# Where weight splits, key tiles and the last token tile's norm and row list stand in the queues of a transformer block

## Chip, cores, metric

One Trainium2 chip; the program runs on one of its cores. The metric is the device time of one execution in microseconds (us). TensorE is called PE (its weight loads PEld), VectorE DVE, ScalarE ACT, GpSimd POOL, SyncE SP.

## The reference

Two blocks over 1024 tokens of width 1024 in float32. The first (gated mixing, a state-space branch, cross attention) is not touched. The second adds to x, in turn: a gated sum of a linear recurrence and a differential attention, a cross attention to 256 memory tokens, and a mixture of 32 experts, two for each token:

```python
q = rope_partial(rms_norm(q, q_norm), cos, sin) * (ATTN_HEAD_DIM ** -0.5)
k = rope_partial(rms_norm(k, k_norm), cos, sin)
sc = einsum('bqhmd,bkhmd->bhmqk', q, k)      # 8 heads, two maps m each
p = softmax(where(mask, sc, NEG_INF))
w = p[:, :, 0] - lam * p[:, :, 1]
o = einsum('bhqk,bkhd->bqhd', w, v)
mixed = sigmoid(g_lru) * y_lru + sigmoid(g_attn) * (o_attn @ w_attn_o)
x = x + mixed @ w_out
x = x + memory_cross_attention_2(x, mem, ...)
h = rms_norm(x, norm_ffn)
# top group of 4, top 2 of its 8 experts per token, then for each expert's tokens
gu = xb @ w_gate_up[e]
y = (silu(gu[:, :512]) * gu[:, 512:]) @ w_down[e]
x = x + weight * y
```

## The kernel before

Every product is made in three matmuls of split operands: a float32 value is split into a high part (ACT copies it, `wh`, `xh`) and a low part (DVE subtracts, `wl`, `xl`). `split` does that; `mm3` issues the three matmuls (lines 173 to 175). So each weight that streams in costs a DMA on SP's queue into a raw buffer, one ACT copy and one DVE subtraction, before PE can use it.

The program is written as one trace; a planner then orders each engine's instructions by their place in the trace among those that its own timing model holds ready. On the chip each engine runs its list in order. `tc.issue_after(ins)` keeps what is issued in its block behind `ins` on the engine of `ins`. Buffers of one tag are a ring, given out in the order of the trace.

**Attention** (`attention`, marks from 690 to 1440 us) works on four pairs of heads, p = 0 to 3. A unit is (pair, query tile, head): `unit_qk` makes two score maps on PE (lines 1504 to 1509), their maxima on DVE and two exponentials on ACT (`e<-sc,st,ss`), `unit_mix` joins the two maps on DVE, `unit_tr` transposes and splits, `unit_pv` multiplies by V. A pair has 16 units, query tiles in the order 0, 7, 1, 6, 2, 5, 3, 4; each step issues the scores of the next unit ahead of the product of this one. In between, `fill` draws on the generator `fillers`: query tiles of the pair, gate units (`gate_unit`, 24 matmuls into `pg`; two units share one weight, streamed by `gate_w`), and `k_tiles` of the next pair, which projects eight key and eight value tiles (`proj`, into `pj`; `norm_rope` normalises a key tile on ACT, DVE and POOL). Weights come by `stream`, each into a raw ring `wr` of two buffers and rings `wh`, `wl` of four; `w2` streams one projection's weight in two parts. A tuple that the generator yields is a hold: nothing more is drawn until the unit loop has put it into `done`. ("k", p + 1) comes when the last unit of pair p has been issued, ("v", p + 1) after that unit's product. Key weights and value weights are streamed ahead of the first hold, and all key tiles are projected behind it.

**The mixer** (cross attention, 1650 to 1860) goes over eight token tiles in steps s1 to s10 written out by hand. For the last tile, `step(9)` writes out the order: s8 in two halves (line 166 adds to x, ACT squares with a sum into `rs3` and `ms`), then loads ahead for the experts, then s9 (transposes for the router; the sum `rs`; `rows`: h = x * norm on DVE, its write to the row buffer x3d on POOL's queue at line 1991, x's write to the output on SP's), then s10 (logits `plg`) and `route`: root of the mean square (two instructions, one on POOL), top group, top two, rank by matmuls, the list of rows per expert (`lst`, cast to `lsti` at line 2150), and behind that the softmax weights and counts. The three gather buffers `xg` are set to zero on POOL in s6 of step 8 (line 2061).

**The experts** (`moe`) take 96 gathered rows each. Six raw loads of 1 MB per expert run on SP through a ring of 15 slots (`moe_ahead`, `moe_load`); `parts` splits half a load, NP = 4 halves ahead of the matmuls. `gather` (line 2215) fetches rows by `lsti` on POOL's queue, `x_turn` transposes them (line 2232), `x_split` splits; `up`, `gated`, `a_turn`, `a_split`, `down`, `scaled` (y on ACT), `scatter` follow. The first four halves are split right after the first three gathers in the trace.

The lines that the change moves:

```python
for t in self.xg:
    nc.gpsimd.memset(t, 0.0)                       # 2061
...
if i == 7 and q:
    last = self.tt(rs3[:, 7:8], rs3[:, 7:8], self.ms[:, 0:1], OP.add)
S[i]["hT"] = hT
with tc.issue_after(last.ins) if i == 7 else nullcontext():
    rows(i)
...
for n in range(NP):
    ahead(n)                                       # moe
```

Of the kernel before, what the change touches and what calls it, by code (L numbers as in the profile page):

```python
# [11 lines left out]
F32 = mybir.dt.float32  # L12
# [4 lines left out]
AF = mybir.ActivationFunctionType  # L17
OP = mybir.AluOpType
AX = mybir.AxisListType
# [5 lines left out]
EPS = 1e-6  # L25
# [104 lines left out]
class Model:  # L130
# [906 lines left out]
    def lru(self):  # L1037
# [3 lines left out]
        self.tab = [D.tile([128, 1024], F32, name=f"ta{i}") for i in range(16)]  # L1041
        self.x0 = None
        self.w4p = self.pool("w4")
# [155 lines left out]
    def attention(self):  # L1199
# [4 lines left out]
        with self.pool("at1") as T1, self.pool("at") as T, \  # L1204
# [9 lines left out]
            alone = [False, 0]  # L1214

            def w2(src):
                return [self.stream(W, src[j], [128, 4, 256]) for j in range(2)]

# [53 lines left out]
            def gate_w(j):  # L1272
                if j < 16 and j not in gst:
                    g, n = gates[j]
                    gst[j] = self.stream(W, A["w_gl2" if g == 0 else "w_ga2"][n], [128, 8, 128])

# [20 lines left out]

            def k_tiles(p):
                wk = w2(A["w_k2"][p])
                wv = w2(A["w_v2"][p])  # L1300
                yield "k", p
                kh = T.tile([128, 4, 1024], F32R, name="kh", tag="kh")
                kl = T.tile([128, 4, 1024], F32R, name="kl", tag="kl")
                V = T.tile([128, 8, 2, 2, 128], F32R, name="V", tag="V")
                KV[p] = [kh, kl, V]
                pend = []

                def finish():
                    j, d = pend.pop(0)
                    pt = transposed(d)  # L1310
                    q = slice(j * 128, j * 128 + 128)
                    self.act(kh[:, :, q], pt, AF.Copy, scale=gcol[:, 1:2])
                    self.stt(kl[:, :, q], pt, gcol[:, 1:2], kh[:, :, q].bitcast(F32), OP.mult, OP.subtract)

                for n in range(8 + 2):
                    if n < 8:
                        o = []
                        yield from proj(wk, n, o)
                        d, _ = norm_rope(o[0], n, True)
                        pend.append((n, d))  # L1320
                    if n == 1:
                        yield "v", p
                    if n > 1:
                        j = n - 2
                        o = []
                        yield from proj(wv, j, o)
                        ps = o[0].rearrange("p (h a) b -> p h (a b)", h=2)
                        self.split(V[:, j, :, 0], V[:, j, :, 1], ps)
                        finish()
                        yield 0.3  # L1330
                        if j == 3:
                            WQ[p] = w2(A["w_q2"][p])

# [147 lines left out]
    def unit_qk(self, unit, QS, KV):  # L1481
# [37 lines left out]
        for m in range(2):  # L1519
            e = T.tile([128, 512 if one else 1024], F32, name="e", tag=f"e{m}{int(one)}", bufs=1)  # L1520
            ev = e[:, 0:W] if one else e[:, 0:W].rearrange("p (a b) -> p a b", a=2)
            self.act(ev, vs[m], AF.Exp, bias=st[:, m:m + 1], scale=rqh[:, m:m + 1], accum=st[:, 2 + m:3 + m])
            es.append(e[:, 0:W])
# [354 lines left out]
    def mixer_tiles(self, x2, XX, xxp, PQ, PT, wcq, wrt, wqp):  # L1878
# [115 lines left out]
        def s9(i):  # L1994
            hT = T.tile([128, 8, 128], F32, name="hT", tag="hT")
            for q in range(2):
                pt = transposes([x2[i][:, (4 * q + a) * 128:(4 * q + a + 1) * 128] for a in range(4)], 4)
                if q:
                    self.act(hT[:, 4:8], pt, AF.Copy)
                else:  # L2000
                    nc.vector.tensor_copy(out=hT[:, 0:4], in_=pt)
                if i == 7 and q:
                    last = self.tt(rs3[:, 7:8], rs3[:, 7:8], self.ms[:, 0:1], OP.add)
            S[i]["hT"] = hT
            with tc.issue_after(last.ins) if i == 7 else nullcontext():
                rows(i)
# [19 lines left out]
        def step(n):  # L2026
# [18 lines left out]
            for f, d in order:  # L2045
                if 0 <= n - d < 8:
# [8 lines left out]
                    if (f, n) == (s6, 8):  # L2055
# [3 lines left out]
                        self.xg = [XG.tile([BLK, 1024], F32, name=f"xg{j}") for j in range(3)]  # L2059
                        for t in self.xg:  # L2060
                            nc.gpsimd.memset(t, 0.0)
                        self.moe_ahead((self.RA, NRA), 2)
# [6 lines left out]
        with self.pool("mt7", side="right") as T, self.pool("po8", space=PSUM) as P2:  # L2069
# [4 lines left out]
            for n in range(1, 11):  # L2074
# [7 lines left out]
                if n in (3, 5, 7, 9):  # L2082

                    self.moe_ahead((self.RA, NRA), 1)

    def route(self, tiles, pl, T, P2, tag):

# [5 lines left out]
        rs = self.rs3[:, ti]  # L2093
        self.ts(rs, rs, 1.0 / 1024, OP.mult, EPS, OP.add)
        self.rsqrt(rs, rs, nb)
        lg = t("lg", 40)
# [52 lines left out]
        if tiles[-1] == 7:  # L2149
            nc.vector.tensor_copy(out=self.lsti, in_=self.lst[:, 0])  # L2150
        yield

        self.tt(ge, lg[:, :, 0:4], bc(m8[:, :, 0, 0:1], 4), OP.subtract)
        self.act(ge, ge, AF.Exp)
        nc.vector.tensor_reduce(out=f[:, :, 1], in_=ge, op=OP.add, axis=AX.X)
        nc.vector.reciprocal(out=f[:, :, 2], in_=f[:, :, 1])
        self.tt(f[:, :, 4], m8[:, :, 1, 1], m8[:, :, 1, 0], OP.subtract)
        self.act(f[:, :, 5], f[:, :, 4], AF.Tanh, scale=0.5)
        self.ts(f[:, :, 6], f[:, :, 5], -0.5, OP.mult, 0.5, OP.add)
        self.ts(f[:, :, 7], f[:, :, 5], 0.5, OP.mult, 0.5, OP.add)  # L2160

        half = f[:, :, 12]
        self.ts(half, rs, 0.5, OP.mult)
        self.tt(f[:, :, 2], f[:, :, 2], rs, OP.mult)
        self.tt(f[:, :, 2], f[:, :, 2], half, OP.mult)
        self.tt(self.val[:, ti, :, 1], f[:, :, 6:8], bc(f[:, :, 2:3], 2), OP.mult)
        nc.vector.tensor_copy(out=self.val[:, ti, :, 2], in_=f[:, :, 12:13].to_broadcast([128, nb, 2]))
        listed(1, 2)
        self.stt(self.dst[:, ti], f[:, :, 10:12], 32.0, f[:, :, 8:10], OP.mult, OP.add)
        for b in range(nb):  # L2170
            self.tt(self.cacc, self.cacc, M[:, b], OP.add)
        if tiles[-1] == 7:

            pc = P2.tile([128, 32], F32, name="pcn", tag=tag)
            nc.tensor.matmul(pc, self.one, self.cacc, start=True, stop=True)
            self.cnt = self.const.tile([128, 32], F32, name="cnt")
            nc.vector.tensor_copy(out=self.cnt, in_=pc)

# [29 lines left out]
    def moe(self):  # L2208
        nc, A, tc = self.nc, self.A, self.tc
        with self.pool("moe") as T, self.pool("mg", bufs=3, space=PSUM) as PG, \  # L2210
# [40 lines left out]
            def gated(u, c):  # L2251

                if c == 0:
                    u["t"] = T.tile([BLK, 512], F32, name="tg", tag="tg", bufs=2)
                    self.act(u["t"], u["pg", 0], AF.Tanh, scale=u["half"])
# [33 lines left out]
            def scatter(u):  # L2289
# [5 lines left out]
                  "xt": xg[e % 3]} for e in range(32)]  # L2295

            for e in range(3):
                gather(U[e])
# [55 lines left out]
            gather(U[3])  # L2354
            for n in range(NP):
                ahead(n)
            for n, (f, e, c, k) in enumerate(work):
# [196 lines left out]
```

## Time and profile before

| what | value |
|---|---|
| median of 3 runs | 2488.14 us (2485.55 to 2493.98) |
| the profiled execution's own time | 2485.62 us |
| its span on the core | 2483.9 us |
| mean granted clock of PE, share of full | 0.983 |
| PE, DVE, ACT, POOL busy | 95%, 70%, 53%, 14% of the span |
| attention | 690 to 1440 us |
| out projection, mixer | 1440 to 1650, 1650 to 1860 us |
| experts | 1860 to 2474 us |

Times in a row of the timeline are microseconds from the span's start, then the duration; what stands in brackets is the idle time of the engine before the instruction and what ended it. "x4" at the end of a row joins four like instructions. A matmul's duration overlaps the next one's. The window rows give the busy time of each engine in a stretch, the number of its instructions, PE's granted clock as a share of 2.4 GHz, the mean busy share of the DMA engines and what they moved.

### The profile page before, as it was taken

What the parts mean: (1) busy time and instruction counts of PE and PEld (TensorE: products, weight loads), DVE (VectorE), ACT (ScalarE), POOL (GpSimd) and SP (SyncE); (2) the same over time, 40 slices, a digit from 0 to 9 for tenths busy, and PEclk for the clock granted to TensorE, in tenths of its full rate; (3) what the DMA queues carried; (4) which work ended last, traced back from release to release, by engine and by line L of the source; (5) the groups of instructions that cost most, each with busy time, mean ns of one, the idle gap of its engine ahead of it and who ended that gap; (6) DMA issues with size and microseconds to landing.
All of it is one profiled execution on the core that took longest, in us unless ns stands there. A gap on an engine that the chain in (4) does not pass through costs nothing. (4 is left out here: it accounts for less than half of the span.)

```text
span 2483.9 us, 35045 instructions
## 1 busy us (share of the span) xinstructions
PE 2355.6 (95%) x13016; PEld 1936.7 (78%) x13016; DVE 1748.2 (70%) x3344; ACT 1314.5 (53%) x2102; POOL 341.5 (14%) x363
## 2 busy tenths in 40 slices
PE   8999989999999999999899899999997999999998
PEld 6888868787888898798798678887885777666765
DVE  9667767677875666666666744235667999898987
ACT  5344532445645455454445432134435888787886
POOL 1011114100021021121121100000011111111111
PEclk9999999999999999999999999999998999999999
DMA  6322353322221111110111456532267999999992
GB/s 222 99 68 67 117 179 127 123 78 84 72 77 39 64 45 42 51 52 35 56 51 40 144 199 221 176 119 77 85 244 271 368 376 373 371 372 359 368 371 66
DMA packets 103838, 394.32 MB, mean 159 GB/s; under 512 B 14129, under 2 KB 33073, under 8 KB 79089
## 3 DMA queue, kind: packets, MB, share of 16 engines
q1 hardware_dynamic: 85008, 335.18, 37.5%
q0 software_dynamic: 18656, 56.88, 7.3%
q8 instruction: 104, 1.70, 0.3%
q14 instruction: 70, 0.57, 0.1%
HBM read 339.07 MB, written 61.31 MB: 161 GB/s over the span
## 5 line engine op out<-in xcount | busy, mean ns | idle before, releaser
L166 DVE TENSOR_TENSOR wl<-raw,wh 128x1024 fp32r<-128x1024 f32 (+1 forms) x496 | 587.7, 1209 | 130.3 <-ACT wh L154 126.1
L154 ACT ACTIVATE wh<-raw 128x1024 fp32r<-128x1024 f32 (+1 forms) x496 | 512.1, 1048 | 250.0 <-PE pj L174 67.2
L173 PE MATMUL pj<-wh,xnh 128*128 128x256 f32 x768 | 222.2, 289 | 2.1 <-ACT tg L154 1.0
L175 PE MATMUL pj<-wh,xnl 128*128 128x256 f32 x768 | 217.2, 283 | 0.0
L174 PE MATMUL pj<-wl,xnh 128*128 128x256 f32 x768 | 217.0, 283 | 0.0
L175 PE MATMUL pg<-wh,xl 128*96 128x512 f32 x512 | 201.3, 393 | 1.6 <-DVE xl L166 1.6
L174 PE MATMUL pg<-wl,xh 128*96 128x512 f32 x512 | 202.6, 396 | 0.0
L173 PE MATMUL pg<-wh,xh 128*96 128x512 f32 x512 | 200.2, 400 | 0.9 <-ACT xh L154 0.9
L173 PEld LDWEIGHTS pj<-wh,xnh 128*128 128x128 f32 x768 | 145.4, 189 | 3.8 <-ACT pc L154 2.5
L174 PEld LDWEIGHTS pj<-wl,xnh 128*128 128x128 f32 x768 | 145.2, 189 | 0.0
L175 PEld LDWEIGHTS pj<-wh,xnl 128*128 128x128 f32 x768 | 145.1, 189 | 0.0
L154 ACT ACTIVATE e<-sc,st,ss 128x1024 f32<-128x1024 f32 (+7 forms) x128 | 105.7, 829 | 54.2 <-DVE st L158 42.4
L178 POOL TENSOR_TENSOR ss<-ss,mhalf 128x4 f32<-128x4 f32 (+1 forms) x68 | 72.7, 1069 | 343.5 <-DVE ss L163 318.4
L173 PE MATMUL pd<-wh,ah 128*96 128x512 f32 x248 | 98.2, 400 | 16.6 <-ACT y L154 16.6
L175 PEld LDWEIGHTS pg<-wh,xl 128*96 128x96 f32 x512 | 83.1, 162 | 38.6 <-DVE xl L166 3.2
L173 PEld LDWEIGHTS pg<-wh,xh 128*96 128x96 f32 x512 | 83.0, 162 | 33.8 <-ACT xh L154 1.3
L174 PEld LDWEIGHTS pg<-wl,xh 128*96 128x96 f32 x512 | 82.8, 162 | 32.4
L173 PE MATMUL pg<-xnh,wh 128*128 128x512 f32 x256 | 104.9, 410 | 0.4 <-ACT kv L154 0.2
L175 PE MATMUL pg<-xnh,wl 128*128 128x512 f32 x256 | 102.6, 401 | 0.0
L173 PE MATMUL pj<-xnh,wh 128*128 128x512 f32 x256 | 102.2, 400 | 0.0
L174 PE MATMUL pg<-xnl,wh 128*128 128x512 f32 x256 | 102.2, 399 | 0.0
L174 PE MATMUL pj<-xnl,wh 128*128 128x512 f32 x256 | 101.2, 396 | 0.0
(998 smaller groups left out, 6327.5 us busy)
## 6 DMA issues: line engine op xcount, KB each, us to landing
raw<-in_w_gu SPq DMA_DIRECT2D x128, 1024.0 KB, 15.3
raw<-in_w_dn SPq DMA_DIRECT2D x64, 1024.0 KB, 15.9
raw<-in_w_out SPq DMA_DIRECT2D x16, 512.0 KB, 4.6
ta<-tg POOLq DMA_DIRECT2D x32, 256.0 KB, 2.5
t<-ta SPq DMA_DIRECT2D x14, 512.0 KB, 3.9
raw<-in_w_ga SPq DMA_DIRECT2D x12, 512.0 KB, 3.7
raw<-in_w_v SPq DMA_DIRECT2D x12, 512.0 KB, 3.5
xraw<-in_xT SPq DMA_DIRECT2D x8, 512.0 KB, 5.8
```

Source lines behind the costliest of these rows:

```text
L154: return self.nc.scalar.activation(out=out, in_=in_, func=func, **kw)
L166: return (eng or self.nc.vector).tensor_tensor(out=out, in0=a, in1=b, op=op)
L173: mm(ps, l[0], r[0], start=start, stop=False)
L174: mm(ps, l[0], r[1], start=False, stop=False)
L175: return mm(ps, l[1], r[0], start=False, stop=stop)
L178: self.nc.gpsimd.tensor_tensor(out=out, in0=in_, in1=self.mhalf[:, :w], op=OP.pow)
```

## The change

In attention, the streams of `w2` and `gate_w` are issued behind the last exponential traced so far (`self.last_exp`), on ACT. The first two key tiles of a pair are projected ahead of the hold ("k", p), the value weights are streamed behind them, and the value hold comes at the third key tile. In the mixer the zeroing of `xg` becomes three ACT copies with scale 0 in s9 of the last tile, whose root is taken there too, ahead of `rows`; `route` skips it for that tile, and what it does behind the list stands behind the list's cast (`self.known`) on DVE. In the experts the first four part splits are issued behind the zeroing (ACT) and the cast (DVE), the ring of raw loads has one slot more, and `tg` one buffer instead of two.

```diff
+            def after_exp():
+                return self.tc.issue_after(self.last_exp.ins) if self.last_exp else nullcontext()
             def w2(src):
-                return [self.stream(W, src[j], [128, 4, 256]) for j in range(2)]
+                with after_exp():
+                    return [self.stream(W, src[j], [128, 4, 256]) for j in range(2)]
...
-                    gst[j] = self.stream(W, A["w_gl2" if g == 0 else "w_ga2"][n], [128, 8, 128])
+                    with after_exp():
+                        gst[j] = self.stream(W, A["w_gl2" if g == 0 else "w_ga2"][n], [128, 8, 128])
...
             def k_tiles(p):
                 wk = w2(A["w_k2"][p])
+                pend = []
+                def project(n):
+                    o = []
+                    yield from proj(wk, n, o)
+                    d, _ = norm_rope(o[0], n, True)
+                    pend.append((n, d))
+                yield from project(0)
+                yield from project(1)
                 wv = w2(A["w_v2"][p])
                 yield "k", p
...
-                for n in range(8 + 2):
+                for n in range(2, 8 + 2):
                     if n < 8:
-                        o = []
-                        yield from proj(wk, n, o)
-                        d, _ = norm_rope(o[0], n, True)
-                        pend.append((n, d))
-                    if n == 1:
+                        yield from project(n)
+                    if n == 2:
                         yield "v", p
-                    if n > 1:
-                        j = n - 2
...
+                    j = n - 2
...
-            self.act(ev, vs[m], AF.Exp, bias=st[:, m:m + 1], scale=rqh[:, m:m + 1], accum=st[:, 2 + m:3 + m])
+            self.last_exp = self.act(ev, vs[m], AF.Exp, bias=st[:, m:m + 1], scale=rqh[:, m:m + 1], accum=st[:, 2 + m:3 + m])
...
-                if i == 7 and q:
-                    last = self.tt(rs3[:, 7:8], rs3[:, 7:8], self.ms[:, 0:1], OP.add)
+                    if i == 7:
+                        self.tt(rs3[:, 7:8], rs3[:, 7:8], self.ms[:, 0:1], OP.add)
+                        root = self.root(rs3[:, 7:8], 1)
+                        for t in self.xg:
+                            self.first = self.act(t, self.ident[0:BLK, 0:1].to_broadcast([BLK, 1024]), AF.Copy,
+                                                  scale=0.0)
             S[i]["hT"] = hT
-            with tc.issue_after(last.ins) if i == 7 else nullcontext():
+            with tc.issue_after(root.ins) if i == 7 else nullcontext():
                 rows(i)
...
-                        for t in self.xg:
-                            nc.gpsimd.memset(t, 0.0)
...
+    def root(self, rs, n):
+        i = self.ts(rs, rs, 1.0 / 1024, OP.mult, EPS, OP.add)
+        self.rsqrt(rs, rs, n)
+        return i
...
-        self.ts(rs, rs, 1.0 / 1024, OP.mult, EPS, OP.add)
-        self.rsqrt(rs, rs, nb)
+        if i0 < 7:
+            self.root(rs, nb)
...
-            nc.vector.tensor_copy(out=self.lsti, in_=self.lst[:, 0])
+            self.known = nc.vector.tensor_copy(out=self.lsti, in_=self.lst[:, 0])
         yield
+        with self.tc.issue_after(self.known.ins) if tiles[-1] == 7 else nullcontext():
...
-                    u["t"] = T.tile([BLK, 512], F32, name="tg", tag="tg", bufs=2)
+                    u["t"] = T.tile([BLK, 512], F32, name="tg", tag="tg")
...
+            self.moe_ahead((T, 1), 1)
             for e in range(3):
                 gather(U[e])
...
-            for n in range(NP):
-                ahead(n)
+            with tc.issue_after(self.first.ins), tc.issue_after(self.known.ins):
+                for n in range(NP):
+                    ahead(n)
```

Under the line `with self.tc.issue_after(self.known.ins) ...` the rest of `route` is indented, unchanged.

## Rows read from the trace of the kernel before

**Rows 1.** The page's busy line: engine, busy us (share of the span), instructions

```profile
PE 2355.6 (95%) x13016; PEld 1936.7 (78%) x13016; DVE 1748.2 (70%) x3344; ACT 1314.5 (53%) x2102; POOL 341.5 (14%) x363
```

**Rows 2.** Windows: attention, head, experts; stretch, us, busy PE PEld DVE ACT POOL, PEclk, DMA, GB/s

```profile
690.00:1440.00 750.00, 714.67 (x4846) 640.53 (x4845) 485.31 (x1215) 371.03 (x759) 120.21 (x139) 0.98 0.16 57
...
1860.00:1883.40 23.40, 8.43 (x69) 7.51 (x67) 12.31 (x51) 3.64 (x8) 4.24 (x5) 0.62 0.67 241
1883.40:2473.50 590.10, 570.54 (x2683) 401.77 (x2682) 532.79 (x564) 484.86 (x571) 86.81 (x60) 1.00 0.93 339
```

**Rows 3.** Waits of PE, 690 to 1440: total us, times, longest us

```profile
PE sc L1504 <- ACT e L154: 10.5, 10, 1.9
```

**Rows 4.** Timeline of ACT in attention, end of pair 0: start, us, operation, [idle before]

```profile
805.19 1.06 ACT L154 ACTIVATE wh<-raw 128x1024 fp32r<-128x1024 f32 x1 [1.61 <-PE pg L174]
...
823.06 1.06 ACT L154 ACTIVATE wh<-raw 128x1024 fp32r<-128x1024 f32 x1 [0.94 <-PE pj L175]
...
835.05 1.06 ACT L154 ACTIVATE wh<-raw 128x1024 fp32r<-128x1024 f32 x1 [5.91 <-PE pg L174]
...
837.46 0.99 ACT L154 ACTIVATE e<-sc,st,ss 128x768 f32<-128x768 f32 x1
...
881.15 0.89 ACT L154 ACTIVATE e<-sc,st,ss 128x640 f32<-128x640 f32 x1 [1.09 <-DVE oss L166]
```

**Rows 5.** Timeline of PE at the end of pair 0

```profile
837.13 0.44 PE L1504 MATMUL sc<-kh,qs 128*128 128x384 f32 x1 [1.88 <-ACT e L154]
...
838.10 0.61 PE L173 MATMUL pg<-xnh,wh 128*128 128x512 f32 x1
...
857.84 0.37 PE L173 MATMUL pj<-wh,xnh 128*128 128x256 f32 x1
...
862.63 0.28 PE L173 MATMUL pj<-wh,xnh 128*128 128x256 f32 x1
...
865.47 0.60 PE L1538 MATMUL pt<-ident,e 128*128 128x128 f32 x4
```

**Rows 6.** Windows: from pair 0's last gate unit to its last exponential

```profile
857.70:882.00 24.30, 20.13 (x144) 18.15 (x144) 18.12 (x51) 10.98 (x25) 2.69 (x4) 0.93 0.10 33
```

**Rows 7.** Timelines of POOL, DVE, ACT and PE at the head of the experts

```profile
1846.40 2.72 POOL L2061 MEMSET xg<- 96x1024 f32 x3
1867.70 0.59 POOL L1991 DMA_DIRECT2D x3d<-h  x1 [18.58 <-DVE rs L163]
...
1877.68 1.10 POOL L2215 DMA_INDIRECT xg<-x3d,lsti  x1 [8.77 <-issue]
...
1864.98 1.22 DVE L166 TENSOR_TENSOR wl<-raw,wh 128x1024 fp32r<-128x1024 f32 x1
1866.12 0.15 DVE L166 TENSOR_TENSOR rs<-rs,ms 128x1 f32<-128x1 f32 x1
...
1868.95 0.20 DVE L166 TENSOR_TENSOR rt_u<-plg,rs 128x36 f32<-128x36 f32 x1 [1.48 <-POOL rs L178]
...
1874.30 0.18 DVE L2150 CAST lsti<-lst 96x32 int32<-96x32 f32 x1
...
1857.75 3.89 ACT L154 ACTIVATE wh<-raw 128x1024 fp32r<-128x1024 f32 x4
...
1863.79 1.03 PE L2018 MATMUL plg<-wrt,hT 128*128 128x36 f32 x8
...
1881.90 1.54 PE L2232 MATMUL pt<-ident,xg 96*128 96x96 f32 x8 [6.19 <-DMA xg<-x3d,lsti]
```

**Rows 8.** The reduce of line 1957: count, duration ns min/median/max, first and last start

```profile
L1957 DVE TENSOR_REDUCE on<-po x8: 1224/1226/2337, 1707.7 to 1846.8; 128x512 f32<-128x1024 f32 x8
```

**Rows 9.** The row writes of line 1991: from issue to landing

```profile
DMA to landing us min/median/max: 2.9/2.9/3.0
```

**Rows 10.** The gathers of line 2215: duration of the issue on POOL, ns

```profile
L2215 POOL DMA_INDIRECT xg<-x3d,lsti x32: 957/1147/3049, 1877.7 to 2391.2; - x32
```

**Rows 11.** Waits of PE among the experts, 2050 to 2475

```profile
PE pd L173 <- ACT y L154: 16.6, 12, 1.7
```

More of the change, by code (lines that the diff above doesn't have):

```diff
@@ L1041, in lru @@
         self.tab = [D.tile([128, 1024], F32, name=f"ta{i}") for i in range(16)]
-        self.x0 = None
+        self.x0 = self.last_exp = None
         self.w4p = self.pool("w4")
@@ L1305, in k_tiles @@
                 KV[p] = [kh, kl, V]
-                pend = []
                 def finish():
@@ L1313, in finish @@
                     self.stt(kl[:, :, q], pt, gcol[:, 1:2], kh[:, :, q].bitcast(F32), OP.mult, OP.subtract)
-                for n in range(8 + 2):
+                for n in range(2, 8 + 2):
                     if n < 8:
-                        o = []
-                        yield from proj(wk, n, o)
-                        d, _ = norm_rope(o[0], n, True)
-                        pend.append((n, d))
-                    if n == 1:
-                        yield "v", p
-                    if n > 1:
-                        j = n - 2
[L1325 to L1332, printed above, removed]
+                        yield from project(n)
+                    if n == 2:
+                        yield "v", p
+                    j = n - 2
+                    o = []
+                    yield from proj(wv, j, o)
+                    ps = o[0].rearrange("p (h a) b -> p h (a b)", h=2)
+                    self.split(V[:, j, :, 0], V[:, j, :, 1], ps)
+                    finish()
+                    yield 0.3
+                    if j == 3:
+                        WQ[p] = w2(A["w_q2"][p])
             def q_tile(p, i):
@@ L2149, in route @@
         if tiles[-1] == 7:
-            nc.vector.tensor_copy(out=self.lsti, in_=self.lst[:, 0])
+            self.known = nc.vector.tensor_copy(out=self.lsti, in_=self.lst[:, 0])
         yield
[L2153 to L2177, printed above, removed]
+        with self.tc.issue_after(self.known.ins) if tiles[-1] == 7 else nullcontext():
+            self.tt(ge, lg[:, :, 0:4], bc(m8[:, :, 0, 0:1], 4), OP.subtract)
+            self.act(ge, ge, AF.Exp)
+            nc.vector.tensor_reduce(out=f[:, :, 1], in_=ge, op=OP.add, axis=AX.X)
+            nc.vector.reciprocal(out=f[:, :, 2], in_=f[:, :, 1])
+            self.tt(f[:, :, 4], m8[:, :, 1, 1], m8[:, :, 1, 0], OP.subtract)
+            self.act(f[:, :, 5], f[:, :, 4], AF.Tanh, scale=0.5)
+            self.ts(f[:, :, 6], f[:, :, 5], -0.5, OP.mult, 0.5, OP.add)
+            self.ts(f[:, :, 7], f[:, :, 5], 0.5, OP.mult, 0.5, OP.add)
+            half = f[:, :, 12]
+            self.ts(half, rs, 0.5, OP.mult)
+            self.tt(f[:, :, 2], f[:, :, 2], rs, OP.mult)
+            self.tt(f[:, :, 2], f[:, :, 2], half, OP.mult)
+            self.tt(self.val[:, ti, :, 1], f[:, :, 6:8], bc(f[:, :, 2:3], 2), OP.mult)
+            nc.vector.tensor_copy(out=self.val[:, ti, :, 2], in_=f[:, :, 12:13].to_broadcast([128, nb, 2]))
+            listed(1, 2)
+            self.stt(self.dst[:, ti], f[:, :, 10:12], 32.0, f[:, :, 8:10], OP.mult, OP.add)
+            for b in range(nb):
+                self.tt(self.cacc, self.cacc, M[:, b], OP.add)
+            if tiles[-1] == 7:
+                pc = P2.tile([128, 32], F32, name="pcn", tag=tag)
+                nc.tensor.matmul(pc, self.one, self.cacc, start=True, stop=True)
+                self.cnt = self.const.tile([128, 32], F32, name="cnt")
+                nc.vector.tensor_copy(out=self.cnt, in_=pc)
```

## The prediction, made before the change was built

> **What bounds the kernel now.** I read the busy line first: PE is busy for 95% of the span, DVE for 70% and ACT for 53% [rows 1]. An average like that hides stages, so the table by stage comes next [rows 2]. Attention (690 to 1440 us) has PE busy for 714.7 of 750 us: 35 us idle in all. The experts (1883.4 to 2473.5) have 570.5 of 590.1. Only the short stretch between them and the mixer is not PE's: from 1860 to 1883.4 PE works 8.4 of 23.4 us. The change touches attention and this stretch, so a gain can come from 35 us at one place and from 15 at the other, never more.
>
> In attention the longest entry in PE's waits is a score tile waiting for an exponential, 10.5 us in 10 times [rows 3]. ACT's timeline shows how this arises at the end of head pair 0: a weight split of the next pair's V (835.05, 1.06 us) sits in front of a unit's two exponentials (the second at 837.46), having waited 5.91 us for matmuls of a gate [rows 4]; PE then stands 1.88 us at 837.13 [rows 5]. That pattern comes three times, at pairs 0, 1 and 2.
>
> At the head of the experts, the chain is: sum of squares, root, logits, row list, gather, transposes, first matmul. The last tile's sum of squares is added at 1866.12, only because DVE has four `wl` parts ahead of it (the last at 1864.98) and ACT four `wh` parts, 3.89 us from 1857.75, ahead of the square; then the multiply of h sits before the root as well. The list ends at 1874.48, but the gather starts at 1877.68; the engine is held by "issue", that is by nothing that the profile names. What it reads besides the list is the row buffer, whose last write was issued at 1867.70; I infer that it waited for it. PE starts at 1881.90 [rows 7].
>
> **The change, part by part.**
>
> *Head of the experts.* (1) The three zeroings of the gather buffers leave POOL (2.72 us at 1846.40). Beside them the DVE reduce of L1957 took 2.34 us, where its others took 1.23 [rows 8]: 1.1 us comes back. ACT takes the three, priced by its like-sized copies at about 1.05 us each [rows 4], in a stretch where it works 3.6 of 23.4 us [rows 2]; they must only end before the gather. (2) With the first four splits behind zeroing and list, the square no longer waits on ACT, nor the sum on DVE: four subtractions less put the sum at 1866.12 - 4 x 1.22 = 1861.2, and I say 1861.9, since the square must end first. The root then is ready near 1863.0, and the next bound is the logits, whose eight matmuls end at 1864.82 [rows 7]. With one semaphore's delay, the first routing step goes from 1868.95 to about 1864.9: -4.0. (3) From there to the list it was 5.5 us (1868.95 to 1874.48). About ten short side operations of DVE, 0.14 to 0.2 each, now follow the list: -1. (4) The row write leaves near 1863.5 instead of 1867.70. Its duration has two bounds: 2.9 us is the landing of the writes that the trace could match [rows 9], and 1877.68 - 1868.29 = 9.4 us is what this one took if the gather waited for it. The middle of the two, 6.2, lands it near 1869.7, no later than the list, at 1869.5; so the list sets the gather. The gather would start near 1870, against 1877.68: -7.7. (5) The `wl` parts, four by 1.22 us [rows 7], now come behind the list at 1869.5 and end near 1874.4, just when the gather's rows are there (4.2 us after its start, 1877.68 to 1881.90 [rows 7]); xl may be 0 to 1.2 late; with (1)'s 1.1 I call it even. Head: **-7.6**, between -3 (write at 9.4 us: 1863.5 + 0.6 + 9.4 = 1873.5, and 1.2 late) and -9.5.
>
> Of gathers beside DVE, the row shows 0.96 to 3.05 us of POOL for one [rows 10], and the first, at 1.10, ran with a nearly idle DVE. The Trainium skill, "SBUF — State Buffer", the part on who interferes with whom, says that subtracting two SBUF operands on DVE (which the splits do) contends with GpSimd's reads, though it doesn't lock it out; by that, the first gather, now beside the four `wl`, would sit at the long end of that row, and the head's gain would be 5.7. No run here shows the overlap yet.
>
> (6) One more raw slot, one `tg` buffer less: weights lead their splits, and `tg` is reused once per expert; PE's waits in that phase name neither [rows 11]. Zero; the cover is the loads' lead. If `tg` bound, it would show as a wait on `tg`.
>
> *Attention.* (7) The streams' ACT splits now stay behind the last exponential traced. The gate weight that was split at 805.19 has to follow the exponential of 837.46 [rows 4], so the gate that starts at 838.10 [rows 5] can't start before that exponential and a split of 1.05. In return the split of 835.05 no longer delays the pair of exponentials, about 1 us. So 837.46 becomes 836.5, its end 837.4, the split's 838.4: +0.3; without the earlier start it is 839.4: +1.3. I take +0.5 a pair, nearer the first, as the split in front is plain in the row. (8) The next pair's key weights, split in two parts, the first at 823.06 [rows 4], are traced after the scores of the pair's last unit, so they must follow that unit's exponential, 881.15 + 0.89 = 882.0 [rows 4]. Two key tiles run there today, from 857.84 and from 862.63, 24 matmuls each, the second until the transposes at 865.47 [rows 5]: 2.8 us for one, so 5.6 us of PE work that can't be there any more. That they stand before the hold in the program does nothing for it: the planner already ran them ahead of the unit that ends the hold. The stretch is 24.3 us with 20.1 of PE, 18.1 of DVE [rows 6]. Without the tiles PE has 14.5 left and DVE about 16 (one tile's normalising is some 2 us), so the chain of exponentials tightens, but not by all of 5.6. Bounds: it tightens fully, 0; not at all, +5.6. I take 4 of 5.6, since 24.3 - 4 is still 4 above DVE's work, as the stretch is now 4 above PE's: loss 1.6, less a little that transposes and mixing fill. +1.5 a pair. (9) The three tiles now in a row share one PSUM buffer, whose copies take 0.4 us: within that term. Pair 3 has no successor, pair 0's start no exponential yet. The query weights' splits move behind exponentials, but the tiles that use them come much later: zero while that holds. Attention: 3 x 2.0 = **+6**, between -9 (the 1.9 us stall and half of the 4.2 us idle vanish in each pair) and +20.
>
> Sum: -7.6 + 6 = -1.6 on the profiled execution's 2485.6 (span 2483.9 and 1.7 around it): 2484.0. That execution is 2.5 below the median of 2488.1, so on the median's footing it is 2486.5. I say **2485**. A measurement of this kernel tells about 0.3%, 7.5 us, from no change.
>
> **The rivals.**
>
> *R1, attention gains too (0.34).* With no split in front, the exponentials come earlier and PE's 4.2 us of idle at each pair's end halves, and the 1.9 us stall with it: 3 x -3 = -9 at best, -3 likely. 2485.6 - 7.6 - 3 to -9: about 2472, range 2468 to 2479. For it: 10.5 us of such waits exist [rows 3]. Against: most stand in the middle of pairs, where no split precedes.
>
> *R2, PE starves at the pair's end (0.17).* The chain of exponentials at 857.7 to 882 doesn't tighten, since it is its own latencies, and PE idles where the two tiles were. +5.6 and 0.5 to 1.3 a pair, some +19: 2485.6 - 7.6 + 19 = 2497. It decides once more than 5 us a pair is lost, from about 2495.6 on. For it: at 881.15 the exponential itself waits for DVE. Against: DVE and PE are shared by tiles and chain now.
>
> *R3, another order of the planner in the experts (0.06).* PE waits 12 times, 1.7 us at most, for y's scaling, 16.6 us in all [rows 11]; another order of ACT's queue there could add half as many or as many again, 8 to 17: at +12, 2485.6 - 7.6 + 6 + 12 = 2496.
>
> *The change does nothing in attention* is 2478.0 on the execution's footing and 2480.5 on the median's, at the forecast's edge to R1; I give it no chance of its own, since splits that start before the exponential of 881.15 are what the edit forbids.
>
> **How the numbers follow.** Forecast 0.43 (within 0.3%), R1 0.34 (faster), R2 and R3 0.23 (slower). The likeliest's own range is 2480.6 to 2495.6. The range 2471 to 2499 takes in most of R1, R2's and R3's centres, and the bounds of head and tiles short of their joint ends.
>
> **What would show it.** In the profile after: the first matmul of the experts some 7.6 us closer to the logits' end; the gather directly behind the list's cast; `wl` and `wh` parts behind it. In attention, gate units 8, 16 and 24 starting right after a split that follows an exponential; the first key tile of pairs 1 to 3 only behind the pair's last exponential; PE's busy time from the gate's end to that exponential about 14.5 us in some 20. Wrong would be: key splits still ahead of the last exponential, a gather that still waits with the list ready, or a stretch of 24 us with 14.5 of PE in it (R2).

## The result, and the profile after

The changed kernel takes 2516.79 us (median of 4 runs, 2512.48 to 2519.76); the kernel before, beside it, 2486.85. The ratio is 1.0119, with a 95% interval of 1.0102 to 1.0136: 1.2% slower, where no measurable change was forecast (2485, range 2471 to 2499).

Where the 30.6 us of the span (2483.9 to 2514.5) went is read by setting the same events of both traces side by side:

| from - to | before | after |
|---|---|---|
| start to the first key projection of attention | 694.7 | 697.2 |
| from there to the end of attention's last transposes | 742.7 | 773.5 |
| from there to the end of the last logits | 427.4 | 425.0 |
| from there to the first expert matmul | 18.6 | 18.5 |
| from there to the end of the last expert matmul | 589.7 | 590.5 |

The 2.5 us at the start lie in unchanged code (that stretch took between 691.8 and 699.1 us in the runs below). Attention lost 30.8, out projection and mixer gained 2.4, and the head of the experts, where -7.6 was forecast, gained next to nothing. The windows of the kernel after, in the columns of [rows 2] and shifted to the same work, say it for the engines:

```profile
692.50:1473.40 780.90, 726.94 (x4846) 642.91 (x4846) 488.06 (x1215) 370.35 (x759) 120.41 (x139) 0.98 0.16 55
1890.90:1914.10 23.20, 7.92 (x67) 7.45 (x66) 13.03 (x48) 4.07 (x9) 8.31 (x6) 0.68 0.77 275
```

Attention issues the same work (4846 matmuls, 759 ACT instructions) in 30.9 us more. PE's idle time grew from 35.3 to 54.0, and the same matmuls were busy 12.3 us longer. PE's mean granted clock is 0.98 in both rows, so the clock does not account for that.

Where the time went shows when each pair's turn is cut in two: from its first exponential to the end of its last, and from there to the first exponential of the next pair. Pair 0, before and then after:

```profile
759.47:882.03 122.56, 116.30 (x715) 100.01 (x714) 78.39 (x198) 58.61 (x126) 13.60 (x17) 0.97 0.13 44
882.03:938.96 56.93, 56.89 (x480) 56.41 (x479) 37.39 (x101) 30.73 (x65) 14.43 (x17) 1.00 0.17 57
```

```profile
761.99:880.35 118.36, 109.60 (x652) 91.54 (x650) 71.98 (x184) 54.75 (x121) 13.06 (x16) 0.99 0.09 32
880.35:948.40 68.05, 65.17 (x541) 64.15 (x542) 44.33 (x115) 34.26 (x68) 15.62 (x18) 1.00 0.21 71
```

The first part became 4.2 us shorter and the second 11.1 us longer: 8.3 us more of PE's work and 2.8 us more of idle time. What moved is 64 projection matmuls (`pj`), two key tiles and two thirds: the first part has 120 instead of 184, the second 456 instead of 392. At pairs 1 and 2 the first part is 2.4 and 3.7 us shorter, the second 12.7 and 12.9 us longer. Together these are 26.4 of the 30.8 us. The rest lies in pair 3, where no key tiles follow; the new place of the key tiles alone, measured below, shows the same 4.3 us there.

The waits of PE in attention, in the form of [rows 3], one row before and three after:

```profile
PE pt L1538 <- DVE e L158: 3.3, 4, 1.5
```

```profile
PE pt L1550 <- DVE e L158: 12.9, 7, 2.5
PE sc L1516 <- ACT e L154: 10.5, 15, 1.3
PE pj L173 <- ACT wh L154: 4.5, 4, 1.4
```

Scores wait for exponentials as long in all as before, 10.5 us. Transposes that wait for the mixing behind the exponentials do so for 12.9 us instead of 3.3. New are key and value tiles (`pj`) that wait for a weight's split, which none did before. ACT at the end of pair 0, to be read against [rows 4]:

```profile
838.88 0.99 ACT L154 ACTIVATE e<-sc,st,ss 128x768 f32<-128x768 f32 x1 [6.43 <-DVE st L158]
...
840.34 0.99 ACT L154 ACTIVATE e<-sc,st,ss 128x768 f32<-128x768 f32 x1
...
841.31 1.06 ACT L154 ACTIVATE wh<-raw 128x1024 fp32r<-128x1024 f32 x1
...
879.47 0.88 ACT L154 ACTIVATE e<-sc,st,ss 128x640 f32<-128x640 f32 x1
880.25 0.19 ACT L154 ACTIVATION_READ_ACCUMULATOR e<-sc,st,ss 128x1 f32 x1
880.34 1.99 ACT L154 ACTIVATE wh<-raw 128x1024 fp32r<-128x1024 f32 x2
...
886.64 1.06 ACT L154 ACTIVATE wh<-raw 128x1024 fp32r<-128x1024 f32 x1 [3.30 <-DMA raw<-in_w_v]
```

The order is what the edit asks for: the gate's split stands behind the pair of exponentials, the two parts of the key weights (880.34) behind the pair's last one. The last row was not foreseen: the value weights' split waits for its own load. The raw ring has two buffers; the key weights held both until their splits, so the value weights' load could only start then, at 883.17, where the kernel before issued it at 825.41 (SP's queue, after and before):

```profile
883.17 1.46 SPq L1634 DMA_DIRECT2D raw<-in_w_v  x2
```

```profile
825.41 4.14 SPq L1622 DMA_DIRECT2D raw<-in_w_v  x2
```

PE of the kernel after in the same stretch:

```profile
874.94 1.11 PE L1550 MATMUL pt<-ident,e 128*128 128x128 f32 x5 [2.47 <-DVE e L158]
881.44 0.38 PE L173 MATMUL pj<-wh,xnh 128*128 128x256 f32 x1 [1.14 <-ACT wh L154]
882.87 0.38 PE L1562 MATMUL po<-V,wth 128*128 128x256 f32 x1 [1.05 <-ACT wth L154]
887.75 0.50 PE L173 MATMUL pj<-wh,xnh 128*128 128x256 f32 x2 [0.70 <-ACT wh L154]
```

The first key tile of pair 1 starts at 881.44 instead of 857.84 [rows 5], though the work around it came up to 3 us earlier. The waits of 1.14 us (for the key split), 1.05 us (for a copy that ACT made behind both key splits) and 0.70 us (for the value split) are the idle time of that second part. At the head of the experts, against [rows 7] (ACT, DVE, POOL, SP, PE):

```profile
1888.71 3.89 ACT L154 ACTIVATE wh<-raw 128x1024 fp32r<-128x1024 f32 x4
...
1894.82 0.22 DVE L166 TENSOR_TENSOR lst<-lst,pls 96x64 f32<-96x64 f32 x1 [2.15 <-PE pls L2165]
1894.96 0.15 DVE L166 TENSOR_TENSOR rs<-rs,ms 128x1 f32<-128x1 f32 x1
...
1896.88 0.20 DVE L166 TENSOR_TENSOR rt_u<-plg,rs 128x36 f32<-128x36 f32 x1 [0.45 <-POOL rs L178]
...
1902.05 0.18 DVE L2171 CAST lsti<-lst 96x32 int32<-96x32 f32 x1
...
1902.50 1.22 DVE L166 TENSOR_TENSOR wl<-raw,wh 128x1024 fp32r<-128x1024 f32 x1
...
1903.70 1.22 DVE L166 TENSOR_TENSOR wl<-raw,wh 128x1024 fp32r<-128x1024 f32 x1
...
1903.20 2.67 POOL L2237 DMA_INDIRECT xg<-x3d,lsti  x1 [5.81 <-ACT rt_f L154]
...
1904.95 2.78 SPq L2209 DMA_DIRECT2D raw<-in_w_gu  x2
...
1911.67 1.54 PE L2254 MATMUL pt<-ident,xg 96*128 96x96 f32 x8 [9.88 <-DMA xg<-x3d,lsti]
```

The list comes sooner behind the logits (1902.23 - 1895.65 = 6.6 us; before 9.7) and the gather a microsecond behind the list (before 3.2). But from the gather's start to the transposes it is 8.5 us, where it was 4.2. Five microseconds were won and four of them lost there; a further one went to the rest of the list, whose matmuls (`pls`, at 1913.01) now ran between the transposes and the first expert matmul.

### The profile page after: what moved, and what is told of

Its sections match the earlier page's. It is cut to its first block, busy times and chain, and to the rows that moved or that the text cites. A ratio compares the mean times of both kernels' runs of the same rounds, so it can differ in the third digit from the quotient of the medians.

```text
span 2514.5 us, 35050 instructions
## 1 busy us (share of the span) xinstructions
PE 2371.1 (94%) x13016; PEld 1941.8 (77%) x13016; DVE 1749.2 (70%) x3344; ACT 1314.7 (52%) x2105; POOL 343.9 (14%) x360
## 5 line engine op out<-in xcount | busy, mean ns | idle before, releaser
L154 ACT ACTIVATE pc<-pj 128x256 f32<-128x256 f32 x96 | 36.3, 382 | 126.5 <-PE pj L175 116.6
```

Of the source, the lines that this page charges most:

```text
L154: return self.nc.scalar.activation(out=out, in_=in_, func=func, **kw)
```

## The experiments

All are measured beside the kernel before. Theory S: the splits tied to the last exponential traced starve PE at the end of each pair. Its rivals are named in the expectations: H (the head has a share), T (the tiles' new place costs), G (the gates' order is a large part), W (keys alone do little).

**Attention's edits alone** (the hunks of `attention`, `k_tiles`, `unit_qk`).

```diff
+    with after_exp():  # w2, gate_w
...
+    yield from project(0)
+    yield from project(1)
     wv = w2(A["w_v2"][p])
     yield "k", p
```

> Theory S (starved pair ends): the whole loss is in attention, where the out projection began 30.9 us later in the changed kernel than before (2.5 us of the shift came earlier, in unchanged code); the attention edits alone give +27 to +31 us, about 2515. Rival H (the head takes a share through DMA contention among the experts): attention alone gives less, +20 to +25, and the rest is missing.

Measured 2523.45, ratio 1.0138 (1.0118 to 1.0157): 36 us slower, above the 27 to 31 expected. Its attention takes 773.5 us, to a tenth what the changed kernel's takes, so the whole loss there is these edits'. It is 6 us slower than the changed kernel because its expert phase took 598.6 us instead of 590.5, with the same code in another order from the planner.

**The head's edits alone** (zeroing, root, `known`, part splits, slot, `tg`).

```diff
+    root = self.root(rs3[:, 7:8], 1)
...
+    with tc.issue_after(self.first.ins), tc.issue_after(self.known.ins):
+        for n in range(NP):
+            ahead(n)
```

> The head's edits alone. Theory S: the list's gain of 3 us is given back by a gather that is slower beside the weight loads and the splits, so -1 to +1 us, about 2486, the first expert matmul 18.5 us behind the end of the logits. Rival H: +4 to +8 us. The forecast of the prediction: -7.6.

Measured 2487.91, ratio 1.001 (0.9995 to 1.0025): no difference. First expert matmul 18.1 us behind the logits.

**The order alone** (`after_exp` without the key tiles' new place) and **the key tiles' new place alone**.

```diff
+    with after_exp():  # first kernel
...
+    yield from project(0)  # second kernel
+    yield from project(1)
     wv = w2(A["w_v2"][p])
     yield "k", p
```

> The splits behind the last exponential, without key tiles ahead of the hold. Theory S: this order alone starves PE, so +24 to +30 us, with no key tile of pairs 1 to 3 before the last exponential of the pair ahead. Rival T (the tiles' new place takes the time): under +12.

> Only the key tiles ahead of the hold (and the value weights' stream behind them, the value hold one tile later), no order between splits and exponentials. Theory S: within 5 us of the kernel before, since the planner already ran two key tiles ahead of the hold. Rival T: +12 or more.

The order alone: 2514.72, ratio 1.0111 (1.0090 to 1.0132). The tiles alone: 2480.45, ratio 0.9961 (0.9945 to 0.9977), faster by 6.9 us where at most 5 were expected. So the change holds a gain of 0.4% and a loss that buries it. With the tiles alone, the stretch at the pair's end, where PE idled 4.2 us [rows 6], is full (windows of that kernel):

```profile
859.50:883.50 24.00, 23.36 (x187) 21.82 (x187) 19.40 (x58) 11.68 (x28) 4.10 (x5) 1.00 0.09 33
```

From a pair's last exponential to the next pair's first it is 54.6 us there at each of three pairs, before 56.4 to 57.7. No split moved: PE still stands 1.88 us ahead of the scores (at 838.92).

In the order without tiles, attention was 24.7 us longer than before (2.8 of them ahead of the first exponential, where no tie acts yet); with them, 30.8. The tiles do nothing for the order: what they need is split behind the exponential that they were to cover.

**Only the gate weights tied**, and **all but the key weights tied** (the latter in the changed kernel).

```diff
-    with after_exp():  # w2 of the first kernel
+    wk = w2(A["w_k2"][p], True)  # second kernel: outside after_exp
```

> Only the gate weights' splits stay behind the last exponential; key, value and query weights are free, key tiles in their old place. Theory S (the loss is the key weights' order): -3 to +6 us against before, the stall of 1.88 us ahead of the scores at the pair's end shorter. Rival G (the gates' order is a large part of the loss): +10 or more.

> The changed kernel with one exception: the key weights' splits are free of the order. Theory S: at least 18 of the 30 us come back, so 2480 to 2499, and key tiles stand ahead of the pair's last exponential again. Rival G: 2505 or more.

Gates: 2504.12, ratio 1.0059 (1.0042 to 1.0076), 14 us, the rival's size. Key weights free: 2500.21, ratio 1.0048 (1.0030 to 1.0066); 17 us came back, a little short of the 18 named, and only 11.8 of them in attention (761.7 against 773.5). So neither is the whole. In the gates' kernel, the stall ahead of the scores did shrink, but two more stood behind it (PE):

```profile
837.31 0.44 PE L1509 MATMUL sc<-kh,qs 128*128 128x384 f32 x1 [0.60 <-ACT e L154]
838.77 0.44 PE L1509 MATMUL sc<-kh,qs 128*128 128x384 f32 x1 [0.33 <-ACT e L154]
841.75 0.87 PE L1543 MATMUL pt<-ident,e 128*128 128x128 f32 x6 [1.31 <-DVE e L158]
```

0.60 + 0.33 + 1.31 = 2.2 us in place of 1.88: the gate unit that ran there now waits for its weight, and nothing covers the mixing. Most of the loss stands later: PE waits 2.46 us for the mixing at 876.24 (before, 1.41 at 873.95), and 16 projection matmuls slip behind the pair's last exponential (408 instead of 392). In all of attention the waits for the mixing are 12.9 us in 7 times, as in the changed kernel. From this stall to the same one of the next pair it is 183.0 us (to 1020.32), before 179.5 (837.13 to 1016.66). With the key weights free, the value weights' splits took their place behind the last exponential. No run ties the value or the query weights alone.

**Only the key weights tied**, all else as before.

```diff
     def w2(src, tied=False):
         with after_exp() if tied else nullcontext():
...
     wk = w2(A["w_k2"][p], True)
```

> Only the key weights' splits stay behind the last exponential; everything else as before. Theory S (PE starves at the pair's end where the key tiles ran): 4 to 6.5 us at each of three pairs, +12 to +20 us; the first key tile of pairs 1 to 3 comes some 23 us later against its neighbours, the chain of exponentials only some 3 us earlier. Rival W (it needs the value and gate weights tied as well): under +6.

Measured 2514.51, ratio 1.0098 (1.0068 to 1.0128): 25 us, above the range of theory S and far from its rival. Attention (694.7 to 1460.3) has 22.9 of them; 2.7 of these lie ahead of the first exponential, where no tie acts yet and the granted clock was 0.95 instead of 1.00. At the three pairs it is 7.7, 5.1 and 6.0 us, 18.7 in all and within the range. Its windows at the end of pair 0:

```profile
858.50:882.50 24.00, 15.32 (x78) 12.29 (x77) 16.64 (x49) 11.80 (x25) 2.60 (x3) 0.76 0.02 6
882.50:905.00 22.50, 22.50 (x170) 22.39 (x170) 16.73 (x42) 11.01 (x22) 6.83 (x8) 0.87 0.38 123
```

PE has 78 matmuls in the first stretch, where [rows 6] have 144, and it idles 8.7 us instead of 4.2. The granted clock was 0.76 of full in it (1.2 GHz for part of it) and 0.87 in the next, where PE had no idle time at all and still only 170 matmuls; before, that next stretch ran at 1.00 with 198:

```profile
882.00:905.00 23.00, 23.00 (x198) 23.00 (x197) 15.52 (x47) 11.55 (x27) 9.27 (x11) 1.00 0.12 47
```

From pair to pair, at the same place as above, it is 187.2 us (838.67 to 1025.84) instead of 179.5. So the starved end costs three times in this kernel: the tiles' own time, the value weights whose load waited for the raw buffers (a split at 887.20 waited 2.92 us for it), and the clock, which was 0.95 behind the last exponential of each of the three pairs. In the changed kernel it was 1.00, 0.94 and 1.00 there.

**The whole change, tied to an earlier exponential**: that of the sixth unit back.

```diff
-    return self.tc.issue_after(self.last_exp.ins) if self.last_exp else nullcontext()
+    return self.tc.issue_after(self.exps[-7].ins) if len(self.exps) >= 7 else nullcontext()
```

> The whole change, but every split of attention stays behind the exponential of the sixth unit back instead of the last one traced. If the loss comes from which exponential it is (theory S: the last one traced belongs to the unit that ends the pair, so that the key tiles can't run beside it): 2472 to 2488, key tiles ahead of the pair's last exponential, PE's half clock after it gone. If any tie of splits to exponentials starves PE: 2500 or more.

Measured 2489.20, ratio 1.0000 (0.9989 to 1.0011): all of the loss is gone. It is a microsecond above the range named, but 27 us below the changed kernel. It is not the tie to exponentials that starves PE but which one is named. Key tiles run from 852.4 again. PE's half clock is not gone, against what I expected: it stands for 3.4 us from 877.8, behind a wait for the mixing of 3.2 us at 876.90. The gain of the tiles alone does not come with this tie. The tiles alone have no such wait there, but that it is the whole reason is not shown.

**The gather at the head.** Two variants of the head's edits: weight loads held on SP's queue, and subtractions held on DVE, until rows have landed.

```diff
+    hold = nc.sync.dma_start(out=scr[:, 0:1], in_=U[0]["xt"][:, 0:1])  # first kernel
+    seen = nc.vector.tensor_copy(out=scr[:, 0:1], in_=U[0]["xt"][:, 0:1])  # second kernel
```

> The head's edits, and the weight loads that the first four part splits release wait on their queue until the first gather has landed (a copy of one column of its rows, on the same queue, ahead of them). If the loads slow the gather: its landing falls from 8.1 us between the gather's start and the transposes (head alone) to about 6, first expert matmul 2 us earlier, 2485 to 2487. If DVE's subtractions beside it do it: nothing changes, 8 us.

> The head's edits, but the first four subtractions on DVE start only when the first gather has landed (behind a DVE copy of one column of its rows), and with them the loads. If subtractions beside the gather slow it: its issue takes 1.1 instead of 2.67 us and it is 4 to 4.5 us from its start to the transposes, first expert matmul 3 us earlier less some 1 us of waiting for the low parts: 2484 to 2487. If not: 8 us remain and the low parts come late, 2489 to 2493.

Measured 2488.07, ratio 0.9995 (0.9980 to 1.0010), and 2486.05, ratio 0.9980 (0.9965 to 0.9995). In both I had put the copy behind the fourth gather, which fills the same buffer, so it waited for that one and not for the first; in the second the low parts came 5.0 us late on PE and ate most of the gain. The first missed its range by a microsecond, the second lies in it. The first expert matmul came 15.8 and 13.5 us behind the logits instead of 18.1, but the expert phases took 594.8 and 595.9 us instead of 592.1. The gather itself can still be read. Head's edits alone (POOL, PE):

```profile
1869.94 2.67 POOL L2225 DMA_INDIRECT xg<-x3d,lsti  x1 [5.81 <-ACT rt_f L154]
...
1877.99 1.54 PE L2242 MATMUL pt<-ident,xg 96*128 96x96 f32 x8 [9.45 <-DMA xg<-x3d,lsti]
```

Loads held, subtractions beside the gather (DVE, POOL, PE):

```profile
1876.88 1.21 DVE L166 TENSOR_TENSOR wl<-raw,wh 128x1024 fp32r<-128x1024 f32 x1
...
1877.92 1.12 POOL L2225 DMA_INDIRECT xg<-x3d,lsti  x1 [7.36 <-issue]
...
1882.17 1.54 PE L2242 MATMUL pt<-ident,xg 96*128 96x96 f32 x8 [7.20 <-DMA xg<-x3d,lsti]
```

That is 8.1 us to the transposes with the head's edits alone and 4.3 with the loads held, where two loads still left at 1880.57 and 1880.95 instead of three from 1871.69 on. With both held it is 4.5 us (1876.95 to 1881.45), issue 1.08. From the end of the issue on it is 5.4 us with the loads and 3.1 without. The run with the earlier tie, which has the head's edits too, shows the two apart the other way: an issue of 1.15, then 5.5 us beside three loads.

The issue beside subtractions took 2.67 and 2.07 us with the head's edits alone, and 1.12 and 2.06 with the loads held; with neither, 1.08 and 0.99. All four end 0.86 to 0.95 us, about the length of an undisturbed issue, behind the end of a subtraction that no other follows at once. For the short one that end came at 1878.09, 0.17 us after the gather's start; for the long one of the changed kernel it came at 1904.92, 1.72 us after it. So by these rows the issue waits until DVE leaves off subtracting.

**A version that beats both**: the tiles alone, the head's edits, and the subtractions held until the first gather has landed (copy ahead of the fourth); the tiles alone with the value weights' splits behind the exponential of the sixth unit back; and the two together.

```diff
     yield from project(0)
     yield from project(1)
-    wv = w2(A["w_v2"][p])
+    with after_exp(7):
+        wv = w2(A["w_v2"][p])
...
+    seen = nc.vector.tensor_copy(out=scr[:, 0:1], in_=U[0]["xt"][:, 0:1])
     x_turn(U[0])
...
+    with tc.issue_after(self.first.ins), tc.issue_after(seen.ins):
+        for n in range(NP):
+            ahead(n)
```

> The key tiles ahead of the hold without any order behind exponentials, the head's edits, and the first four subtractions on DVE only when the first gather has landed, this time placed ahead of the fourth gather. If key tiles gain by themselves (-7) and the gather is slowed by the subtractions and the loads that they release: 2474 to 2480, 4 to 4.5 us from the gather's start to the transposes, first expert matmul 14 to 16 us behind the logits' end.

> The key tiles ahead of the hold, and the value weights' splits behind the exponential of the sixth unit back, where a split has stood in front of a pair of exponentials. If the stall of 1.88 us is that split's: 1 to 2 us less at each of three pairs than with the tiles alone, 2474 to 2480. If a later split or wait takes its place: as the tiles alone, 2480, or above.

> The two kernels before together. If their gains are at separate places: 2470 to 2477.

Measured 2478.24 (ratio 0.9951, 0.9935 to 0.9967), 2477.23 (0.9949, 0.9927 to 0.9971) and 2471.14 (0.9924, 0.9900 to 0.9948). All three lie in their ranges. The third is 0.76% faster than the kernel before and 1.8% faster than the changed one (2471.14 against 2516.79, not run side by side). Its attention takes 727.3 us against 742.7. The stalls of 1.88 us have shrunk to 0.84, as PE and ACT show in it: no split stands in front of the two exponentials, and the one of the value weights follows.

```profile
840.47 0.44 PE L1514 MATMUL sc<-kh,qs 128*128 128x384 f32 x1 [0.84 <-ACT e L154]
...
839.33 0.99 ACT L154 ACTIVATE e<-sc,st,ss 128x768 f32<-128x768 f32 x1 [5.82 <-DVE st L158]
...
840.79 0.99 ACT L154 ACTIVATE e<-sc,st,ss 128x768 f32<-128x768 f32 x1
...
841.76 1.06 ACT L154 ACTIVATE wh<-raw 128x1024 fp32r<-128x1024 f32 x1
```

In the first of the three, the first expert matmul stands 13.4 us behind the logits instead of 18.6; the first gather runs without subtractions beside it (POOL, PE, DVE):

```profile
1863.12 1.07 POOL L2231 DMA_INDIRECT xg<-x3d,lsti  x1 [5.81 <-DVE rt_f L166]
...
1867.50 1.54 PE L2248 MATMUL pt<-ident,xg 96*128 96x96 f32 x8 [2.21 <-DMA xg<-x3d,lsti]
1868.98 0.74 PE L173 MATMUL pg<-wh,xh 128*96 128x512 f32 x1
...
1867.55 4.62 DVE L166 TENSOR_TENSOR wl<-raw,wh 128x1024 fp32r<-128x1024 f32 x4
```

Of these 5.2 us some 5 are lost again among the experts, whose phase took 594.6 us (before 589.7). 2.5 of them are a wait for xl behind the four subtractions; the rest can't be put down to this edit, since the phase took 594 us in runs without it too.

## Why the prediction was wrong, point by point

- *What bounds the kernel* held: PE, and attention as the place where time could be lost. "Never more" was said of gains; no such limit stood on a loss, and none was looked for.
- **Step (8), the key tiles, failed in its size.** The mechanism was right: tiles that can't start before the pair's last exponential, in a stretch with some 15 us of PE work. I let the chain of exponentials tighten by 4 of 5.6 us and took +1.5 a pair. The key weights' tie alone cost 5.1 to 7.7 us at each of three pairs; in the changed kernel, with the other ties, it was 6.9 to 10.3. The tightening was near what I took: 3.6, 5.5 and 6.1 us with the key weights alone, 4.2, 2.4 and 3.7 in the changed kernel. What failed is the 5.6 us, the price of the work that moves behind the exponential: it measured 10.6 to 12.0 and 11.1 to 12.9. At pair 0 of the changed kernel that is 64 matmuls (8.3 us) instead of the 48 of two tiles, and 2.8 us of idle time that the sum had at nothing: for the key split, for a copy queued on ACT behind both key splits, and for the value weights, whose load waits for the raw buffers that the key weights hold (issued at 883.17 instead of 825.41). I had the rings in the description, and counted the ACT splits only, not the loads behind them. With the key weights alone tied the clock comes on top, 0.95 behind each of the three pairs; in the changed kernel only pair 1 shows that.
- **Step (7), the gate weights, failed too**: +0.5 a pair against 3.3, 2.8 and 4.7 us at the three pairs when alone (13.3 us in all of attention). I costed one split's place against one stall (1.88 us), but not what the gate's matmuls had covered: without them PE waits 12.9 us for the mixing in attention instead of 3.3.
- *"That they stand before the hold in the program does nothing for it"* was wrong by itself: with no tie, the new place of the key tiles gains 0.4%. PE's idle at the pair's end went from 4.2 to 0.6 us, the gain that R1 hoped for but not by its mechanism, since the split in front of the exponentials stayed. R1's mechanism shows where the value weights' splits alone are tied to an earlier exponential: 0.84 us of stall instead of 1.88. Only with the tie of the change does the new place do nothing. (R1's -9 is half of 1.9 and 4.2 us at three pairs; the lower bound of attention, worded with all of the 1.9, would be -12.)
- *Head, steps (1) to (5)*: forecast -7.6, measured -0.1, and 2.4 gained in the out projection and the mixer together, where (1) had 1.1. Step (1) held: the reduce took 1.23 us again. What the zeroing slowed was perhaps not the reduce itself: a small scalar operation of DVE just ahead of it (1846.47) took 2.68 us and ended with the zeroing, and the same one took 0.17 us without it (1879.45). Step (2) gave 2.9 of its 4.0 us: the first routing step came 1.2 us behind the logits' end instead of 4.1, not at once. Not the logits bound it but the root, which POOL ended at 1896.84 after 1.46 us (before, 0.59), beside DVE's multiply of h. The sum was held by DVE's queue, behind an addition to the other tiles' list (1894.82). The square still came behind the four splits of ACT (1888.71): the zeroing reads nothing late, so the planner ran it long before (1879.53), and a tie to it held nothing back. Step (3)'s -1 was -0.2 (5.53 to 5.35 us from the first routing step to the list). Step (4) held in the changed kernel, where the gather starts 1.0 us behind the list; with the loads held and with the earlier tie it is 2.5 us, for a reason that no row names. **Step (5) failed:** it took the gather's 4.2 us from an idle moment into one in which four subtractions run and release weight loads; it measured 8.5.
- *The page's rule against the row.* The Trainium skill, "SBUF — State Buffer", the part on who interferes with whom, spoke against this step; the issue at 2.67 us agrees with it. My reading that the subtraction doesn't lock GpSimd out does not fit the rows: the issue ended 0.95 us behind a subtraction's end, and the one of 1.12 us had only 0.17 us to wait. This gave 1.6 us of the four, a little less than the 1.9 that I had named; the loads gave the rest, as the run with loads held shows.
- *R2* had the right side and place, and 2497 for a time, but not the right reason: the chain did tighten, and the loss came behind it. The range stopped at 2499. *R3* did not come to pass in the changed kernel (experts +0.8). In the run of attention's edits the phase was 8.9 us longer, with 3.0 us more in the wait that R3 names (19.6 in 15 times).

## What to carry to other kernels

A tie "behind the last X traced" names an instruction by its place in the program, not by when it runs; where a planner has hoisted work far ahead of its place, such a tie takes the hoisting back, and the filler it stops was what covered the chain. Before such a tie, ask what runs early today because nothing holds it, and what its buffers hold up: an unsplit weight keeps a raw buffer, and so the next load. Naming an exponential six units back took all of the loss away, though the tiles' own gain of 0.4% did not show beside it.

Test bundled edits apart: one part of this change was worth 0.4%, and with a narrower tie and an undisturbed gather 0.76%.

## What the runs showed of the hardware

- A gather of 96 rows took 4.2 to 4.5 us from its start to its first use where no load of 1 MB left in its first 2.6 us (before, loads held, both held, the first of the last three kernels), and 5.5 us once (the third of them). Beside three such loads and the subtractions it took 6.7 (the earlier tie), 8.1 (head alone) and 8.5 us (the changed kernel).
- The gather's issue on POOL took 1.0 to 1.1 us alone. Beside subtractions of two SBUF operands on DVE it ended 0.8 to 0.95 us behind the last of those that ran without a break: 1.12 to 2.67 us in the runs above, and 3.7 us for the fourth gather of two of the last three kernels, which started beside three subtractions.
- TensorE's granted clock: with 8.7 of 24 us idle it was 0.76 in those 24 us and 0.87 in the next 22.5 us, in which PE was busy throughout (key weights tied); with 0.6 us idle in 24 it stayed at 1.00 (tiles alone). In the changed kernel it was 0.91 in the 19.1 us ahead of the end of pair 0's last exponential, 5.9 of them idle, and 1.00 in the 68 us behind.
- The expert phase, with the same code in the kernel before and in that of attention's edits alone, differed by 8.9 us (589.7 and 598.6) in another order of the instructions. Two kernels with one and the same order of all four engines there, the order alone and the value weights behind the exponential of the sixth unit back, took 594.3 and 594.4 us. An edit in one stage can so be misread by that much from the total alone.
